# Which engine computes the lo parts of the input projection's weights: a two-layer decoder trunk on one core

## The chip, the core and the metric

The kernel runs on one core of a Trainium2 chip. The core's engines run side by side, each through its own list of instructions in order: TensorE (PE in the profile, PEld for its weight loads), VectorE (DVE), ScalarE (ACT), GpSimd (POOL) and SyncE (SP), which only issues DMAs here. They wait for each other by semaphores. The metric is the device time of one execution in microseconds. The kernel before took 1199.99 us, the median of three runs between 1198.94 and 1201.08.

## The reference, cut to what matters

A trunk of two layers over 512 tokens of width 1024, in float32. Each layer has one input projection whose 2560 columns are q, k, v (512 each) and the x and gate branches of a recurrent block (512 each):

```
for l in range(2):
    proj = rms_norm(h, g_mix) @ w_in                  # q | k | v | x | gate
    o = diff_attention(rope(q), rope(k), v, lam)      # 4 heads, 2 softmaxes each
    y = rg_lru(conv(x)) * gelu(gate)
    h = h + concat(norm(o), y) @ w_out
    h = h + square(relu(rms_norm(h) @ w_mlp_in)) @ w_mlp_out
    h = h + sigmoid(rms_norm(h) @ w_ple_gate) * (p @ w_ple_proj)
out = rms_norm(h)
```

## The kernel before, in words

Activations lie transposed: 128 features on the partitions, 512 tokens along the free side. To keep float32 precision with TensorE's fp32r type every matrix is split in two: a hi part, the value rounded to fp32r, and a lo part, the value minus hi. A product is three matmuls, hi·hi, hi·lo and lo·hi (`mm3`).

Weights come as chunks of 128 x 1024, 204 of them, in the order of `CHUNKS`. A chunk is loaded by SP into one of four buffers `raw`, ScalarE writes its hi part to one of six buffers `wh`, and VectorE writes the lo part to one of six buffers `wl` (`w_split`). For each layer the list holds four chunks of the x branch ("in", 12 to 15) with the chunk of the small gate matrices between them, then q and k of the four heads ("in", 0 to 7) with four chunks of v ("v") behind the first head's, and four chunks of the gate branch ("in", 16 to 19). Behind them come the output projection, the MLP and the embedding gate. Layer 0's first two chunks are loaded and split in halves by another function, `w_half` with `split`. A chunk of the input projection feeds 24 matmuls of 512 columns.

Beside these chunks VectorE does most of the elementwise work: the residual part `hgl` of the normed activations, the sum of squares `acc`, the convolution `xc`, the recurrence `hs`, rope (`qr`, `q`, `qx`, `kl`), the lo part `vl` of v, the masked maxima of the scores (`pr`, `mx`), and the lo part `at` of the transposed probabilities. TensorE's matmuls of the scores are named `sc`, of the transposes `tr`, of v `pv`, and of every projection `dense`.

GpSimd does little after the constants: per norm one `pow` on a 128 x 4 tile (`rT` for a layer's norm, `orT` for a head's norm), and two small DMAs per head that spread the result over the partitions (`row`, `obc`). `rT` is read by TensorE (`bc<-ident,rT`), whose result all epilogues of the input projection need.

The order of all instructions is set by a planner (`Plan.schedule`): it records them as nodes with dependencies, priorities and an assumed cost per engine, and picks, as a list scheduler does, the next one for each engine. So one changed engine moves instructions of all engines. In the profile every recorded instruction has the line of the planner's `record` (L183), and the tile names tell them apart.

Of the kernel before, what the change touches and what calls it, by code (L numbers as in the profile page):

```python
# [11 lines left out]
F32 = mybir.dt.float32  # L12
# [3 lines left out]
ALU = mybir.AluOpType  # L16
# [359 lines left out]
def chunk_list():  # L376

    c = []
    for l in range(DEPTH):
        c += [("in", l, 12 + m) for m in range(2)]  # L380
        c += [("gates", l, 0)]
        c += [("in", l, 12 + m) for m in range(2, 4)]
        for h in range(NH):
            c += [("in", l, h), ("in", l, 4 + h)]
            if h == 0:
                c += [("v", l, i) for i in range(4)]
        c += [("in", l, 16 + m) for m in range(4)]
        c += [("out", l, m) for m in ORDER]
        for q in range(NQ):
            c += [("up", l, q * KD + m) for m in range(KD)]  # L390
            c += [("down", l, m, q) for m in ORDER]
        c += [("proj", l, 0)]
        c += [("gate", l, m) for m in range(4)]
        c += [("proj", l, 1)]
        c += [("gate", l, m) for m in range(4, 8)]
    return c


CHUNKS = chunk_list()
# [3 lines left out]
def build(ctx: ExitStack, tc: tile.TileContext, given, x, p, pos, w, vec, lamqk, out):  # L403
    rnc = tc.nc
    nc = Plan(rnc, WIN, ('raw', 'wh', 'wl'), given)
    act = nc.scalar.activation
    ve = nc.vector
# [36 lines left out]
    def w_dma(j):  # L444
        while nxt["dma"] <= min(j, len(CHUNKS) - 1):
            i = nxt["dma"]
            t = nc.tile(wrp, [128, 1024], F32, "raw", RAW, "raw")
            nc.sync.dma_start(out=t, in_=w[i])
            raw_t[i] = t
            nxt["dma"] += 1  # L450

    def w_split(j):
        while nxt["split"] <= min(j, len(CHUNKS) - 1):
            i = nxt["split"]
            if CHUNKS[i][0] == "up":
                w_dma(i + 1)
                w_t[i] = pair_parts(raw_t.pop(i), raw_t.pop(i + 1))
                nxt["split"] += 2
                continue
            w_dma(i)  # L460
            raw = raw_t.pop(i)
            hi = nc.tile(wsp, [128, 1024], F32R, "wh", WB, "wh")
            lo = nc.tile(wsp, [128, 1024], F32R, "wl", WB, "wl")
            act(out=hi, in_=raw, func=AF.Copy)
            ve.tensor_tensor(out=lo, in0=raw, in1=hi.bitcast(F32), op=ALU.subtract)
            w_t[i] = (hi, lo)
            nxt["split"] += 1

    def pair_parts(a1, a2):

        lft, rgt = slice(0, S), slice(S, 2 * S)
        s1, s2, s4 = T("s1"), T("s2"), T("s4")
        ve.tensor_tensor(out=s1, in0=a2[:, lft], in1=a2[:, rgt], op=ALU.add)
        ve.tensor_tensor(out=s2, in0=s1, in1=a1[:, lft], op=ALU.subtract)
        ve.tensor_tensor(out=a2[:, lft], in0=a1[:, lft], in1=a2[:, lft], op=ALU.subtract)
        ve.tensor_tensor(out=s4, in0=a1[:, rgt], in1=s2, op=ALU.subtract)
        parts = []
        for src, n in ((a1, 2), (a2, 2), (s2, 1), (s1, 1), (s4, 1)):
            if n == 2:
                hi = nc.tile(wsp, [128, 1024], F32R, "wh", WB, "wh")  # L480
                lo = nc.tile(wsp, [128, 1024], F32R, "wl", WB, "wl")
            else:
                hi, lo = T("sh", F32R), T("sl", F32R)
            act(out=hi, in_=src, func=AF.Copy)
            ve.tensor_tensor(out=lo, in0=src, in1=hi.bitcast(F32), op=ALU.subtract)
            parts += [(hi[:, i * S:(i + 1) * S], lo[:, i * S:(i + 1) * S]) for i in range(n)]
        return dict(zip(("a11", "a12", "s3", "a22", "s2", "s1", "s4"), parts))
# [3 lines left out]
    def take_pair(l, m):  # L491
        i = cur[0]
        assert CHUNKS[i] == ("up", l, m) and CHUNKS[i + 1] == ("up", l, m + 1)
        w_split(i)
        cur[0] += 2
        return w_t.pop(i)

    def take(kind, l, *rest):
        i = cur[0]
        assert CHUNKS[i] == (kind, l, *rest), (CHUNKS[i], kind, l, rest)  # L500
        w_split(i)
        cur[0] += 1
        return w_t.pop(i)

    def ahead(n=LA):
        w_split(cur[0] + n - 1)
        w_dma(cur[0] + n + 1)
# [845 lines left out]
```

## Time and profile before

| | |
|---|---|
| median of three runs | 1199.99 us (1198.94 to 1201.08) |
| the profiled execution's own time | 1199.14 us |
| its span, first to last instruction | 1197.3 us |
| PE busy | 1180.5 us, 99% |
| DVE busy | 968.5 us, 81% |
| ACT busy | 666.0 us, 56% |
| POOL busy | 31.0 us, 3% |
| mean granted TensorE clock | 0.996 |

The profiled execution lies 0.85 us below the median and has 1.84 us outside its span. TensorE looks full from end to end, but its records overlap: a matmul's record lasts longer than the distance to the next one's start, so short waits between matmuls don't show as idle time. VectorE's share of 81% is a mean over stages with different loads; a table by stage stands below.

### The profile page before, as it was taken

The page shows a single profiled execution, that of the slowest core. Times are in us where ns is not written, and L with a number is a line of the kernel's source. Part 1 is how long each engine was busy: PE and PEld are TensorE (multiplying, and loading weights), DVE is VectorE, ACT ScalarE, POOL GpSimd, SP SyncE. Part 2 cuts the span into 40 slices and gives each one's busy share as a digit, 9 for nine tenths or more (in the row PEclk, how much of TensorE's full clock was granted, in tenths as well). Part 3 has the DMA queues.
Part 4 walks back from the last instruction along what each step waited for, and adds up shares of the span by engine and source line. Part 5 has one row for each costly group of instructions (what it writes and reads, how often), then busy time and mean ns, then how long its engine had stood idle before and what let it go on. Part 6 is the DMA issues. An engine that isn't in the chain of part 4 may idle for free.

```text
span 1197.3 us, 17497 instructions
## 1 busy us (share of the span) xinstructions
PE 1180.5 (99%) x6704; PEld 1032.0 (86%) x6704; DVE 968.5 (81%) x1704; ACT 666.0 (56%) x1082; POOL 31.0 (3%) x64
## 2 busy tenths in 40 slices
PE   9999999999999999999999999999999999999996
PEld 6778788988989989988888877899899898898896
DVE  8999988988788678585779899699886787776664
ACT  6887847743634534543459677476355254364352
POOL 1000010000000000000000010000000000000000
PEclk9999999999999999999999999999999999999998
DMA  6323132343333333332322314224332333333202
GB/s 235 110 80 94 39 106 84 104 140 106 106 96 98 106 101 112 105 106 88 94 75 69 115 31 120 77 86 137 107 107 88 106 106 106 93 128 98 88 1 71
DMA packets 35492, 117.35 MB, mean 98 GB/s; under 512 B 4432, under 2 KB 6480, under 8 KB 35408
## 3 DMA queue, kind: packets, MB, share of 16 engines
q1 hardware_dynamic: 34288, 113.59, 30.6%
q0 software_dynamic: 1120, 2.64, 1.0%
q8 instruction: 53, 0.87, 0.3%
q14 instruction: 31, 0.25, 0.1%
HBM read 114.10 MB, written 2.12 MB: 97 GB/s over the span
## 4 chain that ended last, share of the span: by engine, by line
PE 80%; DVE 13%; ACT 3%; issue 2%; DMA 1%; POOL 0%; SPq 0%; POOLq 0%; DVEq 0%; ACTq 0%
PE dense L183 46%; PE up L183 26%; DVE wl L183 2%; PE pv L183 2%; PE pj L183 2%; DVE pr L183 1%; DVE q L183 1%; DVE qr L183 1%; ACT ky L183 1%; PE sc L183 1%; DVE at L183 1%; DVE h L183 1%; DVE qx L183 1%; DVE bl L183 1%; PE gates L183 1%
## 5 line engine op out<-in xcount | busy, mean ns | idle before, releaser
L183 ACT ACTIVATE wh<-raw 128x1024 fp32r<-128x1024 f32 x204 | 213.3, 1054 | 227.2 <-PE dense L183 137.0
L183 DVE TENSOR_TENSOR wl<-raw,wh 128x1024 fp32r<-128x1024 f32 x204 | 247.5, 1218 | 21.1 <-ACT wh L183 20.7
L183 PE MATMUL dense<-ffh,wh 128*128 128x512 f32 x512 | 199.3, 389 | 0.0
L183 PE MATMUL dense<-ffl,wh 128*128 128x512 f32 x512 | 199.3, 389 | 0.0
L183 PE MATMUL dense<-ffh,wl 128*128 128x512 f32 x512 | 199.3, 389 | 0.0
L183 PE MATMUL dense<-hgh,wh 128*128 128x512 f32 (+1 forms) x400 | 151.1, 378 | 0.2 <-DVE vl L183 0.2
L183 PE MATMUL dense<-hgl,wh 128*128 128x512 f32 (+1 forms) x400 | 150.7, 377 | 0.0
L183 PE MATMUL dense<-hgh,wl 128*128 128x512 f32 (+1 forms) x400 | 150.7, 377 | 0.0
L183 DVE TENSOR_TENSOR dn<-dense,obc 128x512 f32<-128x512 f32 x64 | 68.6, 1073 | 56.3 <-PE dense L183 55.5
L183 PEld LDWEIGHTS dense<-ffh,wl 128*128 128x128 f32 x512 | 96.1, 188 | 20.0
L183 PEld LDWEIGHTS dense<-ffh,wh 128*128 128x128 f32 x512 | 96.1, 188 | 19.8
L183 PEld LDWEIGHTS dense<-ffl,wh 128*128 128x128 f32 x512 | 96.1, 188 | 19.5
L183 ACT ACTIVATE sh<-s 128x512 fp32r<-128x512 f32 x96 | 60.5, 631 | 91.3 <-DVE s L183 86.5
L183 PE MATMUL up<-bl,wh 128*128 128x256 f32 x352 | 99.7, 283 | 0.3 <-DVE bl L183 0.3
L183 PE MATMUL up<-bh,wh 128*128 128x256 f32 x352 | 99.8, 284 | 0.2 <-ACT bh L183 0.2
L183 PE MATMUL up<-bh,wl 128*128 128x256 f32 x352 | 99.6, 283 | 0.0
L183 PEld LDWEIGHTS dense<-hgh,wh 128*128 128x128 f32 x400 | 75.7, 189 | 12.5 <-DVE vl L183 0.5
L183 PEld LDWEIGHTS dense<-hgl,wh 128*128 128x128 f32 x400 | 75.8, 189 | 12.2
L183 PEld LDWEIGHTS dense<-hgh,wl 128*128 128x128 f32 x400 | 75.6, 189 | 12.4
L183 PE MATMUL up<-bh,sl 128*128 128x256 f32 x288 | 81.6, 283 | 0.0
L183 PE MATMUL up<-bh,sh 128*128 128x256 f32 x288 | 81.5, 283 | 0.0
L183 PE MATMUL up<-bl,sh 128*128 128x256 f32 x288 | 81.5, 283 | 0.0
(236 smaller groups left out, 2538.3 us busy)
## 6 DMA issues: line engine op xcount, KB each, us to landing
raw<-w SPq DMA_DIRECT2D x204, 512.0 KB, 3.6
obc<-row POOLq DMA_DIRECT2D x10, 256.0 KB, 3.7
h<-x SPq DMA_DIRECT2D x8, 256.0 KB, 5.6
out<-fin SPq DMA_DIRECT2D x8, 256.0 KB, 2.3
w<-w SPq DMA_DIRECT2D x4, 256.0 KB, 4.6
pT<-p SPq DMA_DIRECT2D x4, 256.0 KB, 4.6
lq<-lamqk SPq DMA_DIRECT2D x1, 256.0 KB, 6.6
row<-orT POOLq DMA_DIRECT2D x8, 2.0 KB, 1.7
```

What stands on the lines that cost most here:

```text
L183: d["fn"](*d["args"], **d["kw"])
```

## The change

In `w_split`, the lo part of a chunk of kind "in" or "v" is now computed by GpSimd, and of every other kind by VectorE as before. The operation, its operands and its buffers are the same. Of layer 0's 20 such chunks 18 pass through `w_split`, and all 20 of layer 1: 38 instructions change engine.

```diff
             act(out=hi, in_=raw, func=AF.Copy)
-            ve.tensor_tensor(out=lo, in0=raw, in1=hi.bitcast(F32), op=ALU.subtract)
+            eng = nc.gpsimd if CHUNKS[i][0] in ("in", "v") else ve
+            eng.tensor_tensor(out=lo, in0=raw, in1=hi.bitcast(F32), op=ALU.subtract)
```

GpSimd's list from the last constants to the first head's norm, in the kernel before (`tokC` and `fr` are constants for rope, `rT` layer 0's norm, `orT` a head's):

```order
L183 MEMSET tokC 128x512
L183 MEMSET fr 128x1 x14
L183 TENSOR_TENSOR rT<-me,mhalf 128x4
L183 TENSOR_TENSOR orT<-ome,mhalf 128x4
L183 DMA row<-orT 128x4
L183 DMA obc<-row 128x512
```

The same place in the changed kernel:

```order
L183 MEMSET tokC 128x512
L183 MEMSET fr 128x1 x14
L183 TENSOR_TENSOR wl<-raw,wh 128x1024 x4
L183 TENSOR_TENSOR rT<-me,mhalf 128x4
L183 TENSOR_TENSOR wl<-raw,wh 128x1024 x12
L183 TENSOR_TENSOR orT<-ome,mhalf 128x4
L183 DMA row<-orT 128x4
L183 TENSOR_TENSOR wl<-raw,wh 128x1024
L183 DMA obc<-row 128x512
L183 TENSOR_TENSOR wl<-raw,wh 128x1024
```

Four lo parts now stand ahead of `rT`, twelve between `rT` and the first `orT`, and one between a head's two small DMAs.

VectorE's list in layer 0 where the first scores are due, in the kernel before (`a` and `hs` belong to the recurrence, `kl` to rope's k, the ISA rows are the scores' maxima):

```order
L183 SCALAR_TENSOR_TENSOR ti<-ti,xc 128x512
L183 TENSOR_TENSOR wl<-raw,wh 128x1024 x2
L183 SCALAR_TENSOR_TENSOR a_242<-a_242,tr 128x512
L183 TENSOR_TENSOR kl<-q_260,ky 64x512
L183 TENSOR_TENSOR wl<-raw,wh 128x1024
L183 TENSOR_TENSOR kl<-q_260,ky 64x512
L183 SCALAR_TENSOR_TENSOR vl<-pv,rT,vh 128x512 x3
L183 TENSOR_TENSOR a_242<-a_242,ti 128x512
L183 ISA pr,mx<-sc,mask 128x128
L183 ISA mx 128x1
L183 SCALAR_TENSOR_TENSOR hs<-a,a_242 128x512
L183 SCALAR_TENSOR_TENSOR vl<-pv,rT,vh 128x512
```

The same place in the changed kernel:

```order
L183 TENSOR_TENSOR a_228<-a_228,ti 128x512
L183 TENSOR_TENSOR a_242<-a_242,ti 128x512
L183 SCALAR_TENSOR_TENSOR hs<-a,a_228 128x512
L183 SCALAR_TENSOR_TENSOR hs<-a,a_242 128x512
L183 SCALAR_TENSOR_TENSOR vl<-pv,rT,vh 128x512 x3
L183 ISA pr,mx<-sc,mask 128x128
L183 ISA mx 128x1
L183 ISA pr,mx<-sc,mask 128x128
L183 ISA mx 128x1
L183 ISA pr,mx<-sc,mask 128x256
L183 ISA mx 128x1
L183 SCALAR_TENSOR_TENSOR vl<-pv,rT,vh 128x512
```

Three lo parts of weights that stood just ahead of `vl` are gone from there, the recurrence and `kl` are ahead of it entirely, and the maxima follow it more closely.

## Rows read from the trace of the kernel before

**Rows 1.** Busy us (instructions) of PE, PEld, DVE, ACT, POOL; clock, by stage.

```profile
17.00:60.00 43.00, 41.94 (x196) 34.36 (x195) 41.67 (x120) 31.09 (x45) 2.07 (x1) 1.00 0.39 122
60.00:110.00 50.00, 47.61 (x220) 38.93 (x219) 48.74 (x109) 39.44 (x70) 0.00 (x0) 0.97 0.26 84
110.00:170.00 60.00, 59.37 (x300) 48.13 (x299) 58.20 (x152) 44.92 (x96) 7.14 (x10) 1.00 0.26 76
600.00:640.00 40.00, 40.00 (x184) 32.95 (x183) 31.62 (x48) 27.42 (x39) 1.01 (x1) 1.00 0.18 53
640.00:690.00 50.00, 49.94 (x240) 41.26 (x240) 45.66 (x106) 40.07 (x70) 1.61 (x2) 1.00 0.33 106
690.00:755.00 65.00, 64.51 (x324) 51.93 (x323) 62.99 (x157) 47.33 (x98) 5.43 (x8) 1.00 0.28 78
```

**Rows 2.** The same columns around the hole in TensorE's work in layer 0.

```profile
74.00:76.00 2.00, 0.97 (x6) 0.53 (x4) 1.97 (x3) 1.77 (x3) 0.00 (x0) 1.00 0.84 342
76.00:78.00 2.00, 0.93 (x3) 0.48 (x3) 1.97 (x4) 1.97 (x3) 0.00 (x0) 0.93 0.91 287
78.00:80.00 2.00, 1.84 (x5) 1.58 (x6) 2.00 (x6) 1.98 (x4) 0.00 (x0) 0.50 0.12 47
80.00:82.00 2.00, 2.00 (x8) 1.73 (x7) 2.00 (x10) 1.98 (x2) 0.00 (x0) 0.72 0.00 0
```

**Rows 3.** Chain that ended last, 60 to 90 us: start, us, what.

```profile
70.62 2.34 DVE wl L183 x2
...
74.16 1.13 DVE wl L183
...
76.04 2.08 DVE vl L183 x3
78.12 0.04 issue
78.16 1.22 PE dense L183 x2
```

**Rows 4.** VectorE's groups, 17 to 170 us: busy us, mean ns, idle before.

```profile
L183 DVE TENSOR_TENSOR wl<-raw,wh 128x1024 fp32r<-128x1024 f32 x25 | 30.3, 1215 | 0.0
...
L183 DVE TENSOR_TENSOR qx<-q,qx 64x512 fp32r<-64x512 f32 x8 | 5.5, 686 | 0.2
...
L183 DVE TENSOR_TENSOR q<-dense,cr 128x512 f32<-128x512 f32 x8 | 5.4, 679 | 0.0
...
L183 DVE TENSOR_TENSOR sp<-sp 128x8 f32<-128x8 f32 x1 | 0.2, 160 | 0.0
```

**Rows 5.** GpSimd's groups over the whole span.

```profile
L183 POOL MEMSET tokC<- 128x512 f32 x1 | 0.5, 521 | 0.0
...
masks.py:199 POOL TENSOR_SCALAR_AFFINE_SELECT ident<-ident 128x128 f32<-128x128 f32 x1 | 0.3, 295 | 0.1
```

**Rows 6.** GpSimd's `pow` in order of time: start, us, instruction.

```profile
129.97 1.41 POOL L183 TENSOR_TENSOR orT<-ome,mhalf 128x4 f32<-128x4 f32 x1 [14.56 <-DVE ome L183]
...
556.95 1.03 POOL L183 TENSOR_TENSOR rT<-me,mhalf 128x4 f32<-128x4 f32 x1 [302.74 <-DVE me L183]
...
754.85 1.41 POOL L183 TENSOR_TENSOR orT<-ome,mhalf 128x4 f32<-128x4 f32 x1 [19.73 <-DVE ome L183]
```

**Rows 7.** VectorE beside the first and the last of these.

```profile
129.80 0.69 DVE L183 TENSOR_TENSOR q<-q,qr 128x512 f32<-128x512 f32 x1
...
754.68 0.69 DVE L183 TENSOR_TENSOR s<-raw,s 128x512 f32<-128x512 f32 x1
755.29 1.89 DVE L183 TENSOR_TENSOR sl<-s,sh 128x512 fp32r<-128x512 f32 x3
```

**Rows 8.** TensorE around layer 0's `bc`, in order of time.

```profile
29.82 0.39 PE L183 MATMUL dense<-hgh,wl 128*128 128x512 f32 x1
30.04 0.39 PE L183 MATMUL dense<-hgh,wh 128*128 128x512 f32 x1
31.48 0.49 PE L183 MATMUL bc<-ident,rT 128*128 128x128 f32 x2 [1.05 <-POOL rT L183]
```

## The prediction, made before the changed kernel was run

> **What bounds the kernel now.** I read the page first: TensorE 99% busy, VectorE 81%, and a chain that ended last with TensorE in 80% of it and VectorE in 13%. A share over the span does not tell what VectorE's relief is worth, so I asked for the busy times by stage next. In the input projections VectorE is the fuller engine: 41.67 of 43 us, 48.74 of 50 and 58.20 of 60 in layer 0, and 31.62 of 40, 45.66 of 50 and 62.99 of 65 in layer 1 [rows 1]. TensorE is idle there for 1.06 + 2.39 + 0.63 = 4.08 us in layer 0 and 0 + 0.06 + 0.49 = 0.55 in layer 1. Elsewhere it has no idle time that this change could reach: the start waits for the first loads, and the end for the last norm.
>
> The largest hole is at 74 to 78 us: TensorE busy 0.97 and 0.93 of 2 us, VectorE 1.97 both times, and behind the hole the granted clock is 0.50 for two us and 0.72 for two more, where it was 1.00 before [rows 2]. 0.50 is the lower of the clock's two levels, 1.2 GHz. The chain shows who was late: three lo parts of weights (2.34 and 1.13 us) in the queue ahead of `vl`, and TensorE goes on when `vl` is done [rows 3]. So before this change there is something to win, and it is small.
>
> **What is removed.** 38 lo parts leave VectorE. One lasts 1.215 us [rows 4], but starts of neighbours lie closer: 2.34 for two, 1.13 for one [rows 3], so a lo part occupies the queue for about 1.15 us. That is 18 x 1.15 = 20.7 us in layer 0 and 20 x 1.15 = 23 us in layer 1. If nothing else changed, this would be worth at most what TensorE waits for VectorE: 4.08 + 0.55 us of idle time, plus the slow clock, 2 x 0.50 + 2 x 0.28 = 1.56 us, together 6.2 us. A matmul's record lasts 0.39 us while the next starts 0.22 us later [rows 8], so each wait hides up to 0.17 us, and I allow for as much again: 6 to 12 us in all, not 44.
>
> **What is added.** No row shows GpSimd on a tile of 128 x 1024. The nearest rows: a fill of 128 x 512 takes 0.52 us, twice that is 1.04, and it reads nothing; a select that reads and writes 128 x 128 takes 0.295 us, eight times that is 2.36 [rows 5]. The second reads and writes as a subtraction does, so I take 2.3 us and keep 1.04 and 2.36 as ends. Below zero it can't be: the engine did nothing in these places. A chunk feeds 24 matmuls, 24 x 0.22 = 5.3 us by the starts in [rows 8], so even a lo part that takes 2.3 us and waits for another 1 us before it keeps ahead of TensorE, with six buffers. That cover hides the longer duration. Without it, TensorE would wait for each chunk.
> The Trainium skill, GPSIMD Engine Reference, section "Performance versus the Vector engine", gives 4497 ns for a `tensor_tensor` of 2048 float32; half of it is an estimate of 2.25 us. No run here shows it yet, and with it the sum below would be about 1 us lower.
>
> **What shares the memory.** This term decides. GpSimd's `pow` on 128 x 4 takes 1.03 us where VectorE is idle. In five of its twelve runs of that size it takes longer, and each time VectorE was in an instruction that reads two tensors from SBUF. At 129.97 it takes 1.41 us: VectorE's `q<-q,qr` ends at 130.49, and 131.38 - 130.49 = 0.89 later `pow` is done. At 754.85 it is the same: `s<-raw,s` ends at 755.37, `pow` at 756.26, 0.89 later [rows 6, 7]. So GpSimd waits until VectorE's two-input instruction is over. Whether VectorE waits for GpSimd the same way, these rows can't tell: `pow` reads four elements, and the three `sl` beside it take 1.89 us, as many as without it [rows 7]. A lo part has 2 x 1024 elements to read, which I take to last nearly its whole 2.3 us.
> The Trainium skill, SBUF — State Buffer, section "Who interferes with whom", says it for both sides: a VectorE instruction with two SBUF inputs contends with a GpSimd instruction that reads SBUF, and whichever starts first holds the shared pair for its whole duration. For GpSimd's side the rows agree (0.38 us of waiting at 129.97). For VectorE's side no row shows it, and by the `sl` rows it costs nothing. It speaks against this change.
>
> Price of a VectorE that is held off: bounds are 0 (the `sl` rows) and 2.3 us per lo part (held for all of it). Groups with two SBUF inputs, from `qx<-q,qx` to `sp<-sp`, are 150 of VectorE's instructions in 17 to 170 us without the lo parts, and sum to 83 of 148 us of records [rows 4], 56%. A lo part gets in when such an instruction ends. In 56% of cases the next one is held for all 2.3 us; in the rest VectorE first does instructions with one SBUF input, such as `q<-dense,cr` at 0.68 us, one or two of them, about 1.2 us, and is held for 1.1. 0.56 x 2.3 + 0.44 x 1.1 = 1.8 us. I take that, since `pow` shows the mutual exclusion from one side. Net per lo part: 1.8 - 1.15 = +0.65 us on VectorE.
>
> **The sum.** Layer 0: 18 x 0.65 = 11.7 us, less VectorE's idle time 1.33 + 1.26 + 1.80 = 4.4 [rows 1], is +7.3. Layer 1: five of the 20 fall before the norm is done, under the 8.4 us of idle time of 600 to 640; the other 15 x 0.65 = 9.8, less 4.34 + 2.01 = 6.35, is +3.4. Both layers have VectorE on the path, so I carry this to the end in full. `rT` now stands behind four lo parts on GpSimd, which VectorE's sum of squares also holds up; before, TensorE already waited 1.05 us for `rT` [rows 8]. One lo part in the way more is +2.3. Each new hole of the kind at 74 to 78 us costs 1.56 us of clock; I add two, +3. The `obc` DMA behind one lo part costs nothing: its reader is due at the output projection, behind the gate branch's chunks, and without that cover it would cost 2.3. Sum: 1199.1 (the profiled execution) + 7.3 + 3.4 + 2.3 + 3 = 1215. The profiled execution lies 0.85 us below the median, so a median of 1215 to 1216.
>
> **Rivals.**
> *Relief (faster).* VectorE is not held off. Then its queue is 20.7 and 23 us shorter where it was the fuller engine, `vl` comes three lo parts earlier, the hole at 74 to 78 closes, and with it the clock stays. 6 to 12 us less: 1187 to 1193, say 1190. For it: the `sl` rows, and the fact that the chain in 60 to 90 is VectorE's. Against it: `pow`'s waits. It decides from a hold of under about 0.5 us per lo part.
> *Break-even (same).* The hold is near 1.15 us, as if only the reading phase excluded the other; VectorE's total is what it was, 1197 to 1202, say 1199. For it: `pow` goes on 0.89 us after it got in, and `sl` ran beside that. Against it: it needs a coincidence of two sizes.
> *Full hold.* 2.3 us each: 18 x 1.15 - 4.4 = 16.3, and 15 x 1.15 - 6.35 = 10.9, with the same 5.3 for `rT` and clock: 1232. It is the top of the forecast's own case.
> *GpSimd late.* VectorE always goes first and lo parts wait for several of its instructions, until TensorE waits for `wl`. From the 5.3 us per chunk above this begins at 3 us of waiting for each; one more us for each of 38 would be +38, 1237. The two `pow` got in at the first boundary, so I give it little.
>
> **How the numbers follow.** Forecast (held off, 1203 to 1232) 0.56, relief 0.33, break-even 0.08, GpSimd late 0.03. A measurement of this kernel can tell 0.2%, 2.4 us, from no change. Held off may also end within that bound or below it by a little, which I count with break-even: faster 0.33, same 0.10, slower 0.57. The range takes the relief case but for its best corner and the full hold: 1187 to 1233. The likeliest case by itself has 1203 to 1232.
>
> **What would show it.** Right: VectorE's two-input instructions that stand beside a `wl` of GpSimd have records or gaps 1 to 2.3 us longer, VectorE's busy or waiting time in 17 to 170 stays at 97% or more in spite of 18 fewer instructions, and TensorE has new waits for `acc`, `rT`, `vl`, `at` or `q`. GpSimd's `wl` should take 2.3 us, more where VectorE is in a two-input instruction. Wrong: these VectorE instructions keep their 0.68 us and VectorE shows idle time of some 15 us in layer 0; then relief holds. TensorE waits that end with GpSimd's `wl` would show the last rival.

## The result and the profile after

The changed kernel takes 1240.49 us (median of 1237.27 to 1243.04), the kernel before 1200.18 in the same comparison: a ratio of 1.0337, 95% interval 1.0324 to 1.035. It is slower, as forecast, but by 40 us where 15 were forecast and 33 were the top of the range. The profiled execution took 1238.82 us with a span of 1237.1.

By stage, the columns of [rows 1] for the changed kernel. The three stretches of a layer together hold roughly the same work as in [rows 1] (layer 0's input projection, then layer 1's, which comes 23 us later here); the cuts inside are rough:

```profile
17.00:65.00 48.00, 38.66 (x166) 30.90 (x165) 47.40 (x107) 24.17 (x35) 23.48 (x9) 0.89 0.35 107
65.00:120.00 55.00, 47.74 (x208) 38.37 (x206) 48.36 (x80) 38.68 (x67) 21.54 (x8) 0.94 0.25 77
120.00:190.00 70.00, 65.51 (x333) 53.17 (x332) 67.20 (x173) 49.42 (x107) 12.28 (x11) 1.00 0.24 66
623.00:668.00 45.00, 41.29 (x180) 33.19 (x180) 32.00 (x45) 27.64 (x38) 10.89 (x5) 0.96 0.18 56
668.00:726.00 58.00, 52.33 (x244) 42.80 (x244) 47.50 (x101) 40.82 (x75) 26.41 (x13) 0.97 0.31 96
726.00:790.00 64.00, 59.56 (x302) 48.70 (x301) 61.31 (x145) 43.76 (x91) 10.37 (x8) 1.00 0.25 72
```

TensorE, which had 4.1 us of idle time in layer 0's stretch, has 9.3 + 7.3 + 4.5 = 21.1 here, and 3.7 + 5.7 + 4.4 = 13.8 us in layer 1's, where it had 0.55. The granted clock fell to means of 0.89 and 0.94 in layer 0, where only 60 to 110 had shown 0.97, and of 0.96 and 0.97 in layer 1, where it had been 1.00. VectorE, relieved of 38 instructions, is as busy as before in 17 to 65, and has more idle time later: 6.6 us in 65 to 120, 10.5 in 668 to 726. Over the whole span its busy time has grown from 968.5 to 986.1 us with 38 instructions fewer (busy us, share of the span, instructions):

```profile
PE 1190.0 (96%) x6704; PEld 1038.2 (84%) x6704; DVE 986.1 (80%) x1666; ACT 662.1 (54%) x1080; POOL 127.7 (10%) x102
```

So of the 39.8 us that the span has grown, VectorE is busy for 17.6 and idle for 22.2.

Whom TensorE waited for, us in total, times, longest:

```profile
PE tr L183 <- DVE pr L183: 11.8, 6, 2.7
PE bc L183 <- POOL rT L183: 7.2, 2, 6.1
PE sc L183 <- DVE vl L183: 4.1, 1, 4.1
PE gates L183 <- ACT xch L183: 3.7, 1, 3.7
```

No wait of TensorE ends with a `wl` of GpSimd. The long ones end with VectorE's results, or with results of ScalarE and GpSimd that are made from VectorE's. What had become of VectorE is seen best where GpSimd has one lo part alone, at 704 us; first GpSimd, then VectorE in order of time:

```profile
704.63 2.39 POOL L183 TENSOR_TENSOR wl<-raw,wh 128x1024 fp32r<-128x1024 f32 x1 [6.70 <-ACT wh L183]
```

```profile
704.33 0.66 DVE L183 TENSOR_TENSOR q<-dense,cr 128x512 f32<-128x512 f32 x1
704.92 2.66 DVE L183 TENSOR_TENSOR qr<-qr,sr 128x512 f32<-128x512 f32 x1
707.50 0.55 DVE L183 TENSOR_TENSOR at<-tr,at 128x384 fp32r<-128x384 f32 x1
707.97 0.67 DVE L183 TENSOR_TENSOR q<-q,qr 128x512 f32<-128x512 f32 x1
```

`q<-dense,cr` reads one of its two tensors from PSUM and runs at its 0.66 us; so do all 27 VectorE instructions of that kind that begin while a lo part runs on GpSimd in this trace: none is longer than before. `qr<-qr,sr` reads two from SBUF, begins just after GpSimd's lo part, and has a record of 2.66 us instead of 0.68: it ends 0.56 us after GpSimd is done. The wait is inside the record, so the busy share hides it. At the start of layer 0 even the smallest instructions pay it:

```profile
20.50 2.35 DVE L183 TENSOR_SCALAR ang<-fr,posf 128x16 f32<-128x16 f32 x1
...
23.10 2.38 DVE L183 CAST ah<-ang 128x64 fp32r<-128x64 f32 x1
...
27.42 2.41 DVE L183 TENSOR_SCALAR sp<-sp 128x8 f32<-128x8 f32 x1
...
29.84 2.38 DVE L183 TENSOR_SCALAR pr<-al 128x64 f32<-128x64 f32 x1
...
35.47 0.16 DVE L183 TENSOR_SCALAR me<-msq 128x4 f32<-128x4 f32 x1
```

These four take 0.17 to 0.23 us in the kernel before. They read one tensor from SBUF (`ang` a scalar per partition beside it) and were held all the same. `me` stands behind them in VectorE's queue and comes at 35.47 instead of 29.05; `rT` waits for `me`, and TensorE for `rT`:

```profile
36.86 1.44 PE L183 MATMUL bc<-ident,rT 128*128 128x128 f32 x5 [6.15 <-POOL rT L183]
```

That wait was 1.05 us before [rows 8]. And the clock behind it, in the columns of the first table:

```profile
32.00:36.00 4.00, 0.00 (x0) 0.00 (x0) 4.00 (x27) 0.00 (x0) 0.40 (x2) 0.78 0.67 200
36.00:38.00 2.00, 1.14 (x5) 1.14 (x6) 2.00 (x9) 0.00 (x0) 2.00 (x2) 0.50 0.00 0
38.00:42.00 4.00, 2.64 (x9) 1.72 (x7) 4.00 (x8) 0.00 (x0) 3.44 (x2) 0.62 0.44 119
```

TensorE was idle for these four us and some before, and within them the clock fell to the lower of its two levels; by 38 to 42 it was partly back.

I call a **hold** what a VectorE record has above the median record of the same tiles and shape in the kernel before, where that is over 0.15 us. Summed over the trace of the changed kernel: 34 holds, 57.0 us, 1.50 us per lo part. Ten of them, 16.2 us in sum, are on instructions with one SBUF input.

### The profile page after: what moved, and what is told of

The parts are those of the page before. It is cut to its first block, busy times and chain, and to the rows that moved or that the text cites. A ratio compares the mean times of both kernels' runs of the same rounds, so it can differ in the third digit from the quotient of the medians.

```text
span 1237.1 us, 17565 instructions
## 1 busy us (share of the span) xinstructions
PE 1190.0 (96%) x6704; PEld 1038.2 (84%) x6704; DVE 986.1 (80%) x1666; ACT 662.1 (54%) x1080; POOL 127.7 (10%) x102
## 4 chain that ended last, share of the span: by engine, by line
PE 79%; DVE 13%; ACT 4%; issue 3%; DMA 0%; SPq 0%; POOLq 0%; POOL 0%; DVEq 0%; ACTq 0%
PE dense L183 48%; PE up L183 26%; DVE qr L183 2%; PE pj L183 2%; DVE q L183 2%; DVE pr L183 2%; PE sc L183 1%; DVE xc L183 1%; DVE hs L183 1%; PE av L183 1%; ACT ky L183 1%; PE tr L183 1%; DVE a L183 1%; DVE sp L183 1%; ACT a L183 0%
## 5 line engine op out<-in xcount | busy, mean ns | idle before, releaser
L183 DVE TENSOR_TENSOR wl<-raw,wh 128x1024 fp32r<-128x1024 f32 x166 | 202.5, 1223 | 20.3 <-ACT wh L183 20.2
L183 POOL TENSOR_TENSOR wl<-raw,wh 128x1024 fp32r<-128x1024 f32 x38 | 98.4, 2605 | 165.7 <-ACT wh L183 149.8
```

What stands on the lines that cost most here:

```text
L183: d["fn"](*d["args"], **d["kw"])
```

## Experiments

Two theories stood against each other: HOLD, that GpSimd's reading keeps VectorE waiting, and ORDER, that the planner's new order is the worse one by itself.

**Fill: the changed kernel's order, but GpSimd reads nothing.** The order was planned with the subtraction; the 38 lo parts are left out of the result.

```diff
-            eng.tensor_tensor(out=lo, in0=raw, in1=hi.bitcast(F32), op=ALU.subtract)
+            if given is not None and eng is nc.gpsimd:
+                eng.memset(lo.bitcast(F32), 0.0)
+            else:
+                eng.tensor_tensor(out=lo, in0=raw, in1=hi.bitcast(F32), op=ALU.subtract)
```

> The changed kernel in its own order of instructions, but GpSimd fills the 38 lo parts with zeros (it reads nothing from SBUF); so these lo parts are left out of the result. Theory HOLD (a GpSimd instruction that reads SBUF keeps VectorE's two-input instructions waiting, and TensorE waits for those): no holds, the relief of VectorE remains, so the time falls from 1240 to 1188 to 1196, and VectorE's records of 2.3 us go back to 0.2 to 0.7. Theory ORDER (the planner's new order is the worse one for TensorE, whatever GpSimd does): stays at 1230 to 1245.

Measured: 1193.29 us, 0.9946 of before (0.9931 to 0.9961). So the new order is not the loss: with fills in place of the subtractions it is 6.3 us better than the old one. One place of its trace, GpSimd first, then VectorE:

```profile
621.30 0.96 POOL L183 MEMSET wl<- 128x1024 f32 x1 [7.24 <-PE dense L183]
```

```profile
621.06 0.68 DVE L183 SCALAR_TENSOR_TENSOR ti<-ti,xc 128x512 f32<-128x512 f32 x1
621.66 0.68 DVE L183 TENSOR_TENSOR xp<-dense,rbc 128x512 f32<-128x512 f32 x1
622.26 0.68 DVE L183 TENSOR_TENSOR xcl<-xc,xch 128x512 fp32r<-128x512 f32 x1
```

`ti<-ti,xc` reads two tensors from SBUF beside the fill and keeps its 0.68 us. In the whole trace 17 instructions with two SBUF inputs begin while a fill runs, and none is held. But "no holds" was not met: four instructions with one SBUF input are held. Two are at the start, where the first four fills need nothing and run back to back:

```profile
3.70 3.62 POOL L183 MEMSET wl<- 128x1024 f32 x4
```

```profile
3.63 3.72 DVE L183 COPY sp<-vt 128x4 f32<-128x4 f32 x2 [2.21 <-DMA vt<-vec]
```

The other two stand beside two fills that begin at 28.84 and end at 30.70:

```profile
29.04 1.68 DVE L183 TENSOR_SCALAR sp<-sp 128x8 f32<-128x8 f32 x1
29.16 1.60 DVE L183 TENSOR_SCALAR turn<-turn 128x64 f32<-128x64 f32 x1
```

Two copies of four columns last as long as the four fills, and the two `tensor_scalar` end when the two fills end. So these are held by a GpSimd instruction that only writes, and an instruction with two inputs isn't.
The Trainium skill, SBUF — State Buffer, section "Who interferes with whom", draws that line: two inputs contend with GpSimd's reads alone, copies and `tensor_scalar` in a two-port mode with all of its accesses, and the loser waits to the end. The trace agrees on all three (0.68 us unheld, 3.72 held, 2.66 held).

The four holds sum to 9.9 us, but each pair overlaps, so VectorE stood for about 5. TensorE waited behind the first pair:

```profile
PE dense L183 <- DVE hgl L183: 3.5, 2, 3.1
```

So the 6.3 us are not quite the value of the new order without holds. The fill also needs neither `raw` nor `wh`, so these buffers come free earlier; TensorE waits for no weights in the kernel before either, but no run takes that part out.

**Old order: the order of before, the lo parts on GpSimd.**

```diff
+            eng = nc.gpsimd if CHUNKS[i][0] in ("in", "v") and given is not None else ve
```

> The order of all engines as before the change (planned with VectorE's lo parts), but the 38 lo parts run on GpSimd at their old places. HOLD: VectorE loses some 1.5 us per lo part and is relieved of 1.15, so it is late by about 13 us in all and more where TensorE waits: 1205 to 1225, with holds as in the changed kernel. ORDER: the old order is kept, so 1195 to 1201. If GpSimd being in order mattered (rT behind lo parts), the wait for bc would be as before here, since only few lo parts stand ahead of rT.

Measured: 1240.41 us, 1.0336 (1.0321 to 1.0352), with 32 holds of 57.0 us in sum. That is the loss of the changed kernel in another order of instructions. I had expected 1205 to 1225, since I still credited VectorE's relief. TensorE's waits:

```profile
PE tr L183 <- DVE pr L183: 9.4, 4, 3.7
PE gates L183 <- ACT xch L183: 7.4, 2, 4.4
PE gates L183 <- DVE xcl L183: 3.6, 1, 3.6
PE bc L183 <- POOL rT L183: 2.9, 2, 1.9
```

The wait for `rT` is only 1.9 us here, so the queue at the start is not what makes the total; the same loss has come up elsewhere.

**Again: the kernel before, and GpSimd does the 38 lo parts once more for nobody.**

```diff
+    def twice(fn):
+        def both(**kw):
+            fn(**kw)
+            rnc.gpsimd.tensor_tensor(**dict(kw, out=spare))
+        return both
...
+            if given is not None and CHUNKS[i][0] in ("in", "v"):
+                nc.nodes[-1]["fn"] = twice(nc.nodes[-1]["fn"])
```

> The kernel before, in its order, with all its lo parts on VectorE; GpSimd computes the 38 lo parts once more into a spare tile that nobody reads. Nothing on the path waits for GpSimd but through its queue and the buffers raw and wh that it keeps longer. HOLD: 38 x 1.5 = 57 us of holds without any relief, of which VectorE's idle time takes some: 1235 to 1260. ORDER: 1199 to 1205.

Measured: 1265.88 us, 1.0553 (1.0538 to 1.0569), just above what was expected. 37 holds sum to 72.2 us, and the loss is 66.3: 0.92 us per us of hold. VectorE's idle time of before took next to nothing of it: its busy time rose by 71.4 us, to the 1039.9 below, and the span by 68.5, to 1265.8.

```profile
PE 1200.9 (95%) x6704; PEld 1047.5 (83%) x6704; DVE 1039.9 (82%) x1704; ACT 666.1 (53%) x1082; POOL 134.0 (11%) x102
```

No wait of TensorE, VectorE or ScalarE ends with GpSimd's second computation; SyncE's loads waited for it eight times, 2.2 us at most. The mean granted clock was 0.973, so part of the 0.92 is the clock.

**On VectorE: the changed kernel's order, the lo parts back on VectorE.**

```diff
+            eng = nc.gpsimd if CHUNKS[i][0] in ("in", "v") and given is None else ve
```

> The changed kernel's order on all engines, but the 38 lo parts are issued to VectorE at their places in that order: no holds, and VectorE has 38 x 1.15 = 44 us of work that the planner did not see there. Theory TIME (a microsecond of hold costs what a microsecond of work on VectorE costs; 57 us of holds brought 47 us from the fill run's 1193): 1193 + 44 x 47 / 57 = 1229, 1222 to 1236. Theory PLACE (holds cost more than work of the same length, since they fall on the very instructions that TensorE waits for): 1198 to 1215.

Measured: 1216.3 us, 1.0137 (1.0119 to 1.0155), between the two ranges. From the fill run's 1193.3, 44 us of unplanned work cost 23.0 us, 0.53 per us; 57.0 us of holds cost 47.2, 0.83 per us. Holds are dearer than work of the same length, but not by as much as PLACE had it. Part of the difference is the clock: its mean was 0.996 here and 0.987 with the holds, on spans of 1213.9 and 1237.1 us, that is 4.9 against 16.1 us. At 0.53 the 57.0 us would have cost 30; of the 17 us between that and 47.2 the clock is some 11 by these means, and the rest I did not take apart.

**Quarters: each lo part as four GpSimd instructions.** Here `n` is 256.

```diff
+        def run(out, in0, in1, op):
+            for j in range(0, 1024, n):
+                rnc.gpsimd.tensor_tensor(out=out[:, j:j + n], in0=in0[:, j:j + n], in1=in1[:, j:j + n], op=op)
```

> The changed kernel in its order, each lo part of GpSimd in four instructions of 256 columns. If the exclusion lasts for one GpSimd instruction: no record of VectorE is longer by more than 0.8 us, the longest waits of TensorE shrink, the sum of holds is 40 to 70 us, 1225 to 1245. If it lasts as long as GpSimd has work in its queue: records of VectorE 2.3 us longer as before, 1238 to 1250.

Measured: 1227.07 us, 1.023 (1.0208 to 1.0252). 87 holds, 41.1 us in sum, 0.47 us each and 0.62 at most, as the first of the two theories had it. VectorE at the place where the changed kernel had records of 2.35 and 2.38:

```profile
19.90 0.71 DVE L183 TENSOR_SCALAR ang<-fr,posf 128x16 f32<-128x16 f32 x1
20.52 0.41 DVE L183 TENSOR_TENSOR lq<-lq 128x256 f32<-128x256 f32 x1
20.86 0.71 DVE L183 CAST ah<-ang 128x64 fp32r<-128x64 f32 x1
```

So the exclusion lasts for one GpSimd instruction, and VectorE gets in between two. The pieces themselves, and the whole lo parts of the changed kernel (least, median, most ns):

```profile
L455 POOL TENSOR_TENSOR wl<-raw,wh x152: 716/742/1657, 19.0 to 728.4; 128x256 fp32r<-128x256 f32 x152
```

```profile
L183 POOL TENSOR_TENSOR wl<-raw,wh x38: 2352/2413/4186, 19.6 to 735.3; 128x1024 fp32r<-128x1024 f32 x38
```

**Copy: GpSimd reads one tensor instead of two.** The lo part's buffer gets the hi part.

```diff
+                eng.tensor_copy(out=lo, in_=hi.bitcast(F32))
```

> The changed kernel in its order, GpSimd copies the hi part into the lo part's buffer: one input from SBUF instead of two (the 38 lo parts are so left out of the result, and hi stands in their place). If reading is what excludes VectorE: holds in the number of the changed kernel (some 35), each as long as the copy, 1.0 to 1.3 us, so some 25 us in sum, 1205 to 1222. If only an instruction with two inputs excludes: as the fill run, 1190 to 1197.

Measured: 1202.28 us, 1.002 (1.0011 to 1.003): below the first range, above the second. One input holds VectorE too, but there were only 23 holds of 15.1 us in sum, 0.66 each, and the copy takes 1.05 us:

```profile
L183 POOL CAST wl<-wh x38: 1037/1046/1967, 18.9 to 700.2; 128x1024 fp32r<-128x1024 f32 x38
```

**Only v: 8 of the 38 lo parts on GpSimd.**

```diff
-            eng = nc.gpsimd if CHUNKS[i][0] in ("in", "v") else ve
+            eng = nc.gpsimd if CHUNKS[i][0] in ("v",) else ve
```

> Only the 8 lo parts of v's chunks on GpSimd, planned so. If each lo part on GpSimd costs the same, (1240.5 - 1199.5) / 38 = 1.08 us: 8 x 1.08 = 8.6, 1208 (1203 to 1213). If the price grows with their number (the early ones of layer 0 and the heads' ones are the dear ones): 1197 to 1203.

Measured: 1210.75 us, 1.0091 (1.0071 to 1.011), 11.2 us for 8 lo parts, 1.4 each, where the mean of all 38 is 1.08. Eight holds sum to 14.2 us. So the price per lo part is not lower with few of them. These eight have their own plan and their own places, so the run does not tell number from place.

**Aware: the planner knows of the exclusion.** It does not plan a lo part on GpSimd and a VectorE instruction with all inputs in SBUF at the same time.

```diff
+                    if d["port"]:
+                        s = max(s, held["dve" if e == "pool" else "pool"])
...
+            if d["port"]:
+                held[e] = end
```

> The planner is told of the mutual exclusion: an instruction of VectorE whose inputs all lie in SBUF and a lo part on GpSimd are not planned at the same time (and a lo part costs 2.40 us instead of 2.33). HOLD, with the plan's wrong assumption as the amplifier: TensorE has other work where VectorE is held, 1200 to 1215, holds of VectorE still 40 to 60 us in sum. HOLD alone without such an amplifier: 1225 to 1240. ORDER says nothing definite.

Measured: 1228.64 us, 1.0238 (1.0221 to 1.0255), with 32 holds of 54.5 us. That lies in the second range, of HOLD alone: a plan that knows of the exclusion wins back 12 us of 40, and the sum of holds stays nearly as it was. TensorE did not find other work for the rest.

In the runs in the changed kernel's order the time rises with the holds in sum: copy 15.1 us and 1202.3, quarters 41.1 and 1227.1, all lo parts 57.0 and 1240.5. The steps from the fill's 1193.3, its own four holds counted as nothing, are 0.60, 0.82 and 0.83 us per us of hold. No version with all lo parts computed beats the kernel before.

## Why the prediction was wrong in size

**The mechanism** was right in the main. VectorE's instructions with two SBUF inputs are held beside a GpSimd lo part, by the whole rest of it; with a fill in place of the subtraction the loss is gone, with GpSimd's lo parts added to the kernel before it is back. It was too narrow: ten of the 34 holds fell on instructions with one SBUF input. The `sl` records that I had as the lower bound [rows 7] did not show the hold; that `pow` reads too little for it is likely, but no run shows it.

**The duration** of 2.3 us was right (median 2.41). The estimate of 2.25 us would have lowered my sum by 1.7 us, not by about 1; nothing hangs on it. That TensorE never waits for a lo part itself was right, and so was `obc` at no cost: no wait of TensorE ends with it.

**The hold per lo part** was set at 1.8 us and measured at 1.50. This error went the other way.

**The step that failed** is the one behind it: "Net per lo part: 1.8 - 1.15 = +0.65 us on VectorE", carried through as the loss, less VectorE's idle time. It took an instruction less on VectorE, and an idle microsecond on VectorE, to be worth as much as a hold costs. The runs: the relief with hardly any holds is worth 6.3 us in all (fill), not 43.7; holds without relief cost 0.92 us per us (again). On VectorE itself the net was not far off: 38 x 0.65 = 24.7 us forecast, 17.6 us more busy time measured. What failed is that the time does not follow this net: it grew by 40. As two prices, 57.0 x 0.83 - 6.3 gives the 41.0 us measured by construction, since both prices come from the fill run; again, quarters and copy have 0.92, 0.82 and 0.60 us per us of hold. My own text had the warning: a few lines earlier it valued the same relief at "6 to 12 us in all, not 44". And the idle time, 10.75 us credited, absorbed nothing that shows: it grew by 22.2 us, and in the run again it fell by 2.9. That VectorE's holds fell where TensorE waited for the held instruction, and its idle time lay where it waited for others, fits TensorE's waits; no run takes it apart.

**Two smaller terms** were too small. `rT` was set at +2.3 and waited 5.1 us more, since `me` stood behind four held instructions of 0.2 us each, which I had not counted as held: they have one SBUF input, and my rule took only those with two. The clock was set at +3 for two holes; mean clocks of 0.996 on 1197.3 and 0.987 on 1237.1 us are 4.8 and 16.1 us, so the term was 11, part of it under idle time that is counted anyway.

**The rivals.** Relief's size was right (fill: 6.3 us), its condition did not hold. Full hold had the right hold for about half of the VectorE instructions that were hit (15 of 34 above 2.0 us), and still took off the relief and the idle time, so it ended at 1232 where 1240 was measured. Break-even's hold of 1.15 us was under the 1.50 measured. GpSimd late did not occur: ScalarE waited twice for a lo part, 5.3 us in all, and TensorE never. I had said that VectorE would stay at 97% or more in 17 to 170; it did in 17 to 65 (47.40 of 48) and not behind it (48.36 of 55): a held engine also releases others later, and can then wait for them.

## What to carry to other kernels

An offload has two prices that must not be netted on the relieved engine: what the relief is worth, which is only the waits that end with that engine, and what the new work does to instructions that others wait for. Before moving two-input elementwise work from VectorE to GpSimd, look at which VectorE instructions will stand beside it: if they read all their inputs from SBUF and TensorE waits for them, a us of hold can cost nearly a us (0.6 to 0.9 here). Read the records' lengths against the same group before, for a held instruction counts as busy.

## What the runs showed of the hardware that I had not expected

- A one-input VectorE instruction of very few elements is held as fully as a big one: `ang`, 128x16, 2.35 us instead of 0.23, and two copies of 128x4 for 3.72 us beside four GpSimd fills that read nothing.
- The exclusion ends with each instruction: with lo parts in four pieces the mean hold is 0.47 us instead of 1.68 (57.0 / 34), although GpSimd had as many columns to do.
- GpSimd waits too: `wl` takes 2.35 us at least and 4.19 at most. In the longest, two `xcl` of VectorE ran from 50.11 to 51.39, the next instruction with two SBUF inputs began at 51.31 and took 2.88 us, and the lo part ended at 53.65, 2.34 us after 51.31: so it had let several go first.

```profile
49.46 4.19 POOL L183 TENSOR_TENSOR wl<-raw,wh 128x1024 fp32r<-128x1024 f32 x1 [8.02 <-ACT wh L183]
```

```profile
50.11 1.28 DVE L183 TENSOR_TENSOR xcl<-xc,xch 128x512 fp32r<-128x512 f32 x2
51.31 2.88 DVE L183 SCALAR_TENSOR_TENSOR xc<-xp,vt,xc 128x510 f32<-128x510 f32 x1
```
